# Layer 0 of a hybrid decoder: the second query chunk multiplied between the logits of two heads, and the output weights of the recurrent half split behind the heads' exponentials

## The chip, the cores and the metric

The kernel runs on one core of a Trainium2 chip. Its time is the device time of one execution in microseconds, the median of three runs. The core has TensorE (matrix products, into PSUM banks of 128x512 fp32), VectorE, ScalarE and GpSimd (elementwise work) and SyncE, which issues the DMAs. Each engine works through its own queue in order and waits at semaphores for the others.

## What is computed

A two-layer trunk over 512 positions of width 1024, in fp32. The change touches layer 0 alone:

```python
proj = x @ w_in          # 512 + 512 + 512 + 64 + 64 + 256 + 64 + 4 columns
xr, yr, q, k, v, iq, ik, iw = jnp.split(proj, split_points, axis=-1)
xr = causal_depthwise_conv(xr, conv_w, conv_b)
rec = rg_lru(xr, ...) * jax.nn.gelu(yr)          # recurrent half, 512 wide
att = dsa_attention(q, k, v, iq, ik, iw)         # 8 heads of 64; 128 best keys of each query
return jnp.concatenate([rec, att], axis=-1) @ w_out
```

`dsa_attention` scores all keys with the indexer (`iq`, `ik`, `iw`), keeps 128 of them for each query, and takes a causal softmax with a position bias over these. `rg_lru` is a gated linear recurrence over time. Then come a layer norm, a squared-ReLU MLP with a gated input embedding, and a second layer norm; layer 1 has latent attention in place of the hybrid mixer.

## The kernel before

Activations stand transposed, features on partitions and 512 positions along the free axis. A product that must be nearly fp32 is made of three matmuls in a faster fp32 format: weights and activations are split into a high and a low part (`split`, L88: ScalarE rounds to the high part, VectorE or GpSimd subtracts for the low part), and `mm3` adds high x high, high x low and low x high. `wload` (L92) loads a 1 MB chunk of weights into one of two `wraw` buffers and splits it into one of two `whi`/`wlo` pairs; `ahead` moves the split forward in the planner's priorities.

`mixer0` is layer 0's mixer. The input projection runs in chunks of 256 columns. Chunks 4 to 7 go through `gemm_full` (L591), which multiplies the raw fp32 weights by the raw `y` without any split, 16 matmuls for a chunk (the trace shows each as two records). Chunks 4 and 5 are the gelu branch; chunk 6 holds the queries of heads 0 to 3, chunk 7 those of heads 4 to 7. `ev3` (L670) evacuates a PSUM tile of two heads: for each head a ScalarE copy (L469), a VectorE difference (L470) and a second ScalarE copy (L673). `topk` (L542) runs on VectorE beside the chunks and gives the masks `mb`. `recurrence` (L638) and `recurrence_end` (L647) finish the recurrent half; the latter takes four blocks of 128 channels, two by two: (0, 1) before the attention, (2, 3) within it. A block of it is six VectorE instructions and a scan, one ScalarE scaling (L653), a cast to `mixed` (L89) and a subtraction on GpSimd (L90).

`attention` (L422) is a pipeline over the heads. In step i it traces the logits of head i, the transposes of head i - 2, the output of head i - 3, and then calls `after(i)`. `Head.logits` (L367) goes over four query blocks, 3 down to 0: two matmuls for each (L704, L705), then on VectorE one instruction that scales, masks and finds the extremum (L380). Blocks 1 and 0 share a PSUM bank, so the matmuls of block 0 wait until block 1 is masked. Then ScalarE takes four exponentials with their sums (L384), VectorE the reciprocals (L386), and GpSimd multiplies (the normalisation, L388, four instructions). The tiles of the sums have two buffers, so head i + 2's exponentials wait for head i's normalisation. `transposes` (L391) turns the probabilities by TensorE and splits them; `output` (L406) multiplies by the values.

`after(1)` traces `recurrence_end((2, 3))`, with its VectorE instructions queued behind head 1's last mask (`tc.issue_after`). `after(4)` and `after(6)` trace `gemm_t` of output-weight chunks 0 and 1, the recurrent half's: each loads and splits its chunk (on GpSimd for the low part) and makes 48 matmuls into the spare pair of PSUM banks (`ps_g`), which `ev_rec` adds to `y`. Chunks 2 and 3 follow after the attention.

A planner orders each engine's queue when the program is built: it runs through an estimate of time, and whenever an engine is free it issues the instruction of the highest priority that is ready. Priority is the order of tracing, moved by `ahead`. On the chip the queues then keep that order, whatever the real durations are.

Of the kernel before, what the change touches and what calls it, by code (L numbers as in the profile page):

```python
# [11 lines left out]
AF = mybir.ActivationFunctionType  # L12
OP = mybir.AluOpType

P = 128
# [38 lines left out]
def hybrid_kernel(ctx: ExitStack, tc: tile.TileContext, a: dict, out: bass.AP):  # L54
    nc = tc.nc
    uid = [0]

    def nm(s):
        uid[0] += 1
        return f"{s}_{uid[0]}"  # L60
# [18 lines left out]
    def ps_tile(tag=None):  # L79
        if tag is None:  # L80
            tag = TURN[turn[0] % 6]
            turn[0] += 1
        return psum.tile([P, S], F32, tag=tag, bufs=BANKS[tag], name=nm("ps"))

    def ps_g():
        return ps_tile("g")

    def split(hi, lo, src, act=None, sub=None):  # L88
        (act or nc.scalar.copy)(hi, src)  # L89
        (sub or nc.vector.tensor_sub)(lo, src, f(hi))  # L90

    def wload(dram, idx, n=2048, pieces=2, sub=None, raw=None, ahead=30):  # L92

        hi = wp.tile([P, 2048], F32R, tag="whi", name=nm("whi"))
        lo = wp.tile([P, 2048], F32R, tag="wlo", name=nm("wlo"))
        if raw is None:
            raw = wp.tile([P, 2048], F32, tag="wraw", name=nm("wraw"))
            nc.sync.dma_start(raw[:, :n], dram[idx, :, :n])
        m = n // pieces
        with tc.high_priority(ahead):  # L100
            for i in range(pieces):
                c = slice(i * m, (i + 1) * m)
                split(hi[:, c], lo[:, c], raw[:, c], sub=sub)
        return hi, lo

    def mm3(ps, whi, wlo, xhi, xlo, start, stop):
        nc.tensor.matmul(ps, whi, xhi, start=start, stop=False)  # L107
        nc.tensor.matmul(ps, whi, xlo, start=False, stop=False)  # L108
        nc.tensor.matmul(ps, wlo, xhi, start=False, stop=stop)  # L109

    ALL, HALVES = slice(0, S), (slice(0, H), slice(H, S))

    def gemm_t(dram, idxs, xs, evac, kk=8, nt=2, lead=0, ps=ps_tile, sub=None, loaded=None,
               halves=(), tail=0, ahead=30):

        tiles = {}  # L120

        def part(g, c, w, kn, cs=ALL):
            ktot = kk * len(idxs[g])
            for k, n in kn:
                key = g, n, cs.start
                if key not in tiles:
                    tiles[key] = ps()
                kx = c * kk + k
                hi, lo = xs[kx]
                o = slice((k * nt + n) * P, (k * nt + n + 1) * P)  # L130
                mm3(tiles[key][:, cs], w[0][:, o], w[1][:, o], hi[:, cs], lo[:, cs],
                    kx == 0, kx == ktot - 1)
                if kx == ktot - 1:
                    evac(g * nt + n, tiles[key], cs)

        first, last = 0, len(idxs) - tail
        byn = [(k, n) for n in range(nt) for k in range(kk)]
        byk = [(k, n) for k in range(kk) for n in range(nt)]
        if lead:
            w = loaded or [wload(dram, idxs[g][0], sub=sub, ahead=ahead) for g in range(2)]  # L140
            first = 2
            for cs in HALVES if "lead" in halves else (ALL,):
                for k in range(lead):
                    for g in range(2):
                        part(g, 0, w[g], [(k, n) for n in range(nt)], cs)
                for g in range(2):
                    kn = (byk, byn)[g]
                    part(g, 0, w[g], [t for t in kn if t[0] >= lead], cs)
        for g in range(first, last):
            for c, idx in enumerate(idxs[g]):  # L150
                part(g, c, wload(dram, idx, sub=sub, ahead=ahead), byn)
        if tail:
            w = {(g, c): wload(dram, idx, sub=sub, ahead=ahead) for g in range(last, len(idxs)) for c, idx in enumerate(idxs[g])}
            for cs in HALVES:
                for g in range(last, len(idxs)):
                    cn = [(c, n) for n in range(nt) for c in range(len(idxs[g]))]
                    for c, n in cn if cs.start == 0 else sorted(cn):
                        part(g, c, w[g, c], [(k, n) for k in range(kk)], cs)
# [201 lines left out]
    class Head:  # L360
# [6 lines left out]
        def logits(self):  # L367
            p = self.pool
            ps = {t: ps_tile("s") for t in "ABC"}
            sb = {t: p.tile([P, WIDTH[t]], F32, tag="l" + t, bufs=3 - (t in self.few), name=nm("l")) for t in "ABC"}  # L370
            mn = p.tile([P, NB], F32, tag="mn", name=nm("mn"))
            sums = p.tile([P, NB], F32, tag="sums", name=nm("sums"))
            L = {}
            for blk in (3, 2, 1, 0):
                t, c0 = S_AT[blk]
                n = (blk + 1) * P
                m = max(n, 2 * P)
                self.s_mm(ps[t][:, c0:c0 + m], blk, m)
                L[blk] = sb[t][:, c0:c0 + n]
                self.masked = nc.vector.tensor_tensor_reduce(  # L380
                    out=L[blk], in0=ps[t][:, c0:c0 + n], in1=self.mask(blk, n), scale=-self.scale,
                    scalar=-LOWEST, op0=OP.add, op1=OP.min, accum_out=mn[:, blk:blk + 1])
            for blk in (3, 2, 1, 0):
                nc.scalar.activation(L[blk], L[blk], AF.Exp, bias=mn[:, blk:blk + 1],  # L384
                                     scale=-1.0, accum_out=sums[:, blk:blk + 1])
            nc.vector.reciprocal(sums, sums)  # L386
            for blk in (3, 2, 1, 0):
                nc.gpsimd.tensor_scalar(L[blk], L[blk], sums[:, blk:blk + 1], 1.0, op0=OP.mult, op1=OP.mult)  # L388
            self.L = L
# [66 lines left out]
    def mixer0(mixed):  # L456
        with pool("m0", 1) as m0, pool("m0s") as sc:
# [4 lines left out]
            def scr():  # L462
                return sc.tile([P, S], F32, tag="s", bufs=1, name=nm("s"))
# [58 lines left out]
            for blk in (3, 2, 1):  # L522
                n = (blk + 1) * P
                isc[blk] = xp.tile([P, n], F32, tag=f"isc{blk}", bufs=1, name=f"isc{blk}")
                for h in range(4):
                    ps = ps_tile()
# [61 lines left out]
            gl = rp.tile([P, D], F32R, tag="gl", bufs=1, name="gl")  # L588
            split(gh, gl, gr[:, :D], sub=nc.gpsimd.tensor_sub)

            def gemm_full(idxs, evac):  # L591

                for g, idx in enumerate(idxs):
                    raw = wp.tile([P, 2048], F32, tag="wraw", name=nm("wraw"))
                    nc.sync.dma_start(raw, a["w_in"][idx])
                    for n in range(2):
                        ps = ps_tile()
                        for k in range(KT):
                            o = (k * 2 + n) * P
                            nc.tensor.matmul(ps, raw[:, o:o + P], y[k], start=k == 0, stop=k == KT - 1)  # L600
                        evac(2 * g + n, ps, ALL)
# [45 lines left out]
            def recurrence_end(ns):  # L647
                for n in ns:
                    T, rc, st, nt = rg[n], rcs[n], gy[n], scr()
                    nc.vector.scalar_tensor_tensor(nt, T, 1.0, rc, op0=OP.add, op1=OP.mult)  # L650
                    nc.vector.scalar_tensor_tensor(rc, nt, 2.0, rc, op0=OP.subtract, op1=OP.mult)
                    nc.vector.tensor_mul(T, T, rc)
                    nc.scalar.activation(T, T, AF.Copy, scale=2.0, bias=1.0)  # L653
                    nc.vector.tensor_mul(st, st, rc)
                    nc.vector.scalar_tensor_tensor(st, st, -1.0, ix[n], op0=OP.mult, op1=OP.mult)
                    nc.vector.tensor_tensor_scan(ix[n], T, st, 0.0, op0=OP.mult, op1=OP.add)
                    nc.vector.tensor_mul(gy[n], ix[n], gelu[n])
                    mixed[n] = new_h(n)
                    split(mixed[n][0], mixed[n][1], gy[n], sub=nc.gpsimd.tensor_sub)
# [12 lines left out]
                    head_halves(q1[:, 2 * n + j], ps, j)  # L672
                    nc.scalar.copy(q2[0:64, 2 * n + j], ps[64 * j:64 * j + 64])  # L673

            gemm_full([6, 7], ev3)
            recurrence()
            recurrence_end((0, 1))

# [4 lines left out]
            def ev_rec(n, ps, cs):  # L683
                nc.vector.scalar_tensor_tensor(y[n], y[n], ALPHA, ps, op0=OP.mult, op1=OP.add)

            def after(i):
                if i == 1:
                    with tc.issue_after(heads[1].masked.ins):
                        recurrence_end((2, 3))
                if i in (4, 6):  # L690
                    g = (i - 4) // 2
                    gemm_t(a["w_out0"], [[g]], mixed, lambda n, ps, cs: ev_rec(n + 4 * g, ps, cs), kk=4, nt=4,
                           ps=ps_g, sub=nc.gpsimd.tensor_sub)

            def mask(blk, n):
                return tri[:, 3 * P:] if blk == 0 else mb[blk]
# [1 line left out]
            heads = []  # L698
# [401 lines left out]
    for layer in range(2):  # L1100
        mixed = [None] * KT
# [111 lines left out]
```

## Time and profile before

| | us |
|---|---|
| time before, median of 3 runs | 1281.77 |
| lowest and highest of them | 1279.61, 1283.0 |
| the profiled execution's own time | 1281.88 |
| span of its trace | 1279.7 |
| TensorE busy | 1233.8 (96%) |
| VectorE busy | 936.5 (73%) |
| ScalarE busy | 685.3 (54%) |
| GpSimd busy | 161.7 (13%) |

The span runs from the first to the last instruction; 2.2 us lie around it. Busy times are of one profiled execution. Matmuls overlap one another in the records (a 128x512 matmul is shown as 0.39 us and the next starts 0.23 us later), so busy TensorE is not TensorE at its peak, and the spacing of starts is what a matmul costs. The granted clock is a share of 2.4 GHz; 0.50 is 1.2 GHz. Layer 0's mixer takes the first 210 us or so; the attention runs from about 122 to 205.

### The profile page before, as it was taken

How to read it: one execution, taken by the hardware profiler on the slowest of the kernel's cores; microseconds unless marked ns; L12 is line 12 of the kernel's file. 1: busy time of each engine (PE TensorE's matmuls, PEld its weight loads, DVE VectorE, ACT ScalarE, POOL GpSimd, SP SyncE). 2: the span in 40 equal slices, each digit the busy share in tenths (PEclk: the TensorE clock that was granted, in tenths of full speed). 3: DMA queues.
4: the chain of work that ended last, by engine and by line, in shares of the span. 5: the costliest groups of instructions: out<-in, count | busy, mean ns of one | idle time of the engine just before them, and what ended most of it. 6: DMA issues, size and time to landing. Idle time of an engine off the chain costs nothing.

```text
span 1279.7 us, 18724 instructions
## 1 busy us (share of the span) xinstructions
PE 1233.8 (96%) x7240; PEld 1066.5 (83%) x7240; DVE 936.5 (73%) x1833; ACT 685.3 (54%) x1260; POOL 161.7 (13%) x186
## 2 busy tenths in 40 slices
PE   7999699999999999999899999999999999999998
PEld 6744488989899899898787878899898998988987
DVE  5997677899667575585848888769985574855857
ACT  5593564756426245263366989636563262452633
POOL 0502651000000000000544443200000000000000
PEclk9999699999999999999998999999999999999999
DMA  6202112113223323233122110213232231332301
GB/s 215 100 34 95 69 34 83 67 66 132 100 99 103 119 75 123 72 103 131 35 71 99 34 34 1 83 66 100 99 100 99 99 132 66 100 130 68 132 33 67
DMA packets 20921, 110.96 MB, mean 87 GB/s; under 512 B 2464, under 2 KB 6560, under 8 KB 8640
## 3 DMA queue, kind: packets, MB, share of 16 engines
q1 hardware_dynamic: 20736, 109.18, 24.9%
q8 instruction: 56, 0.92, 0.3%
q0 software_dynamic: 96, 0.59, 0.2%
q14 instruction: 33, 0.27, 0.1%
HBM read 107.66 MB, written 2.10 MB: 86 GB/s over the span
## 4 chain that ended last, share of the span: by engine, by line
PE 76%; DVE 13%; ACT 6%; POOL 2%; issue 1%; DMA 1%; ACTq 0%; SPq 0%; POOLq 0%; DVEq 0%
PE ps L783 24%; PE ps L107 14%; PE ps L108 14%; PE ps L109 14%; DVE mb L551 2%; DVE m L550 2%; ACT whi L89 1%; PE ps L397 1%; ACT l L384 1%; POOL l L388 1%; PE ps L417 1%; PE ps L907 1%; PE ps L908 1%; PE ps L906 1%; POOL wlo L90 1%
## 5 line engine op out<-in xcount | busy, mean ns | idle before, releaser
L89 ACT CAST whi<-wraw 128x1024 fp32r<-128x1024 f32 (+3 forms) x154 | 129.9, 882 | 148.9 <-PE ps L108 113.9
L108 PE MATMUL ps<-al,whi 128*128 128x512 f32 (+1 forms) x544 | 206.4, 379 | 0.0
L107 PE MATMUL ps<-ah,whi 128*128 128x512 f32 (+1 forms) x544 | 206.4, 379 | 0.0
L109 PE MATMUL ps<-ah,wlo 128*128 128x512 f32 (+1 forms) x544 | 205.3, 377 | 0.0
L107 PE MATMUL ps<-hh,whi 128*128 128x256 f32 (+1 forms) x432 | 147.3, 344 | 8.2 <-ACT hh L89 6.6
L109 PE MATMUL ps<-hh,wlo 128*128 128x256 f32 (+1 forms) x432 | 145.5, 341 | 1.4 <-DVE wlo L90 0.8
L108 PE MATMUL ps<-hl,whi 128*128 128x256 f32 (+1 forms) x432 | 146.7, 341 | 0.1
L90 POOL TENSOR_TENSOR wlo<-wraw,whi 128x512 fp32r<-128x512 f32 (+2 forms) x46 | 73.3, 1614 | 484.4 <-ACT whi L89 452.6
L90 DVE TENSOR_TENSOR wlo<-wraw,whi 128x1024 fp32r<-128x1024 f32 (+1 forms) x108 | 116.1, 1107 | 16.5 <-ACT whi L89 16.3
L783 PE MATMUL ps<-xt,whi 128*128 128x256 f32 x680 | 124.6, 284 | 0.6 <-DVE u L802 0.6
L108 PEld LDWEIGHTS ps<-al,whi 128*128 128x128 f32 x544 | 102.8, 189 | 20.1 <-DVE al L90 1.2
L107 PEld LDWEIGHTS ps<-ah,whi 128*128 128x128 f32 x544 | 102.8, 189 | 19.6 <-ACT ah L89 1.1
L109 PEld LDWEIGHTS ps<-ah,wlo 128*128 128x128 f32 x544 | 102.7, 189 | 18.6 <-issue 0.5
L783 PEld LDWEIGHTS ps<-xt,whi 128*128 128x128 f32 x680 | 106.0, 192 | 1.0 <-DVE u L802 0.8
L748 ACT CAST whi<-wraw 128x1024 fp32r<-128x1024 f32 (+1 forms) x43 | 36.0, 836 | 130.1 <-PE ps L108 97.1
L874 DVE TENSOR_TENSOR y<-y,ps 128x512 f32<-128x512 f32 (+1 forms) x52 | 33.3, 644 | 94.2 <-PE ps L109 94.1
L107 PEld LDWEIGHTS ps<-hh,whi 128*128 128x128 f32 x432 | 82.5, 192 | 18.0 <-ACT hh L89 7.9
L783 PE MATMUL ps<-xt,wlo 128*128 128x256 f32 x340 | 96.2, 283 | 0.0
L109 PEld LDWEIGHTS ps<-hh,wlo 128*128 128x128 f32 x432 | 82.5, 192 | 10.9 <-DVE wlo L90 2.0
L108 PEld LDWEIGHTS ps<-hl,whi 128*128 128x128 f32 x432 | 83.0, 192 | 9.8 <-DVE hl L90 0.9
L783 PE MATMUL ps<-hh,wlo 128*128 128x256 f32 x260 | 73.5, 283 | 0.0
L783 PE MATMUL ps<-hl,whi 128*128 128x256 f32 x260 | 73.5, 283 | 0.0
(338 smaller groups left out, 2983.5 us busy)
## 6 DMA issues: line engine op xcount, KB each, us to landing
wraw<-in_mlp_w SPq DMA_DIRECT2D x64, 1024.0 KB, 4.8
wraw<-in_w_out SPq DMA_DIRECT2D x8, 1024.0 KB, 4.7
wraw<-in_w_gate SPq DMA_DIRECT2D x8, 1024.0 KB, 4.8
wraw<-in_w_in SPq DMA_DIRECT2D x6, 1024.0 KB, 4.8
wraw<-in_w_ukv SPq DMA_DIRECT2D x4, 1024.0 KB, 4.8
wraw<-in_w_in SPq DMA_DIRECT2D x16, 128.0 KB, 4.0
y<-in_xT SPq DMA_DIRECT2D x8, 256.0 KB, 3.8
wraw<-in_w_proj SPq DMA_DIRECT2D x2, 1024.0 KB, 4.8
```

The source lines that it names most:

```text
L89: (act or nc.scalar.copy)(hi, src)
L90: (sub or nc.vector.tensor_sub)(lo, src, f(hi))
L107: nc.tensor.matmul(ps, whi, xhi, start=start, stop=False)
L108: nc.tensor.matmul(ps, whi, xlo, start=False, stop=False)
L109: nc.tensor.matmul(ps, wlo, xhi, start=False, stop=stop)
L384: nc.scalar.activation(L[blk], L[blk], AF.Exp, bias=mn[:, blk:blk + 1], scale=-1.0, accum_out=sums[:, blk:blk + 1])
L388: nc.gpsimd.tensor_scalar(L[blk], L[blk], sums[:, blk:blk + 1], 1.0, op0=OP.mult, op1=OP.mult)
L550: nc.vector.max(out=m8, in_=src)
L551: nc.vector.match_replace(out=w, in_to_replace=m8, in_values=src, imm_value=LOWEST)
L748: nc.scalar.copy(hi, src)
L783: nc.tensor.matmul(o, u[:, c], v, start=start and k == n == 0, stop=k == 3 and n == 2, skip_group_check=True)
L874: nc.vector.tensor_add(yn, yn, ps[:, cs])
```

## The change

Chunk 7 is taken out of the call in front of `recurrence()`. It is multiplied in `after(1)` instead, traced behind the logits of head 1 and ahead of `recurrence_end((2, 3))`, and into the spare pair of PSUM banks. `gemm_full` gets the number of its first chunk and the banks as parameters for that. The output-weight chunks 0 and 1 are loaded and split in `after(1)` and `after(3)`; their ScalarE casts are queued behind the last exponential of head 1 and of head 3 (the instruction kept in `self.exp`), with `ahead=0`. `after(4)` and `after(6)` keep the same 48 matmuls each, in the same order.

```diff
-                nc.scalar.activation(L[blk], L[blk], AF.Exp, bias=mn[:, blk:blk + 1],
+                self.exp = nc.scalar.activation(L[blk], L[blk], AF.Exp, bias=mn[:, blk:blk + 1],
                                      scale=-1.0, accum_out=sums[:, blk:blk + 1])
...
-            def gemm_full(idxs, evac):
-
-                for g, idx in enumerate(idxs):
+            def gemm_full(idxs, evac, first=0, bank=ps_tile):
+
+                for g, idx in enumerate(idxs, first):
...
-                        ps = ps_tile()
+                        ps = bank()
...
-            gemm_full([6, 7], ev3)
+            gemm_full([6], ev3)
             recurrence()
             recurrence_end((0, 1))
...
             def after(i):
                 if i == 1:
+                    gemm_full([7], ev3, 1, ps_g)
                     with tc.issue_after(heads[1].masked.ins):
                         recurrence_end((2, 3))
+                if i in (1, 3):
+                    with tc.issue_after(heads[i].exp.ins):
+                        wo.append(wload(a["w_out0"], len(wo), sub=nc.gpsimd.tensor_sub, ahead=0))
                 if i in (4, 6):
                     g = (i - 4) // 2
-                    gemm_t(a["w_out0"], [[g]], mixed, lambda n, ps, cs: ev_rec(n + 4 * g, ps, cs), kk=4, nt=4,
-                           ps=ps_g, sub=nc.gpsimd.tensor_sub)
+                    for n in range(4):
+                        ps = ps_g()
+                        for k in range(4):
+                            o = slice((k * 4 + n) * P, (k * 4 + n + 1) * P)
+                            mm3(ps, wo[g][0][:, o], wo[g][1][:, o], *mixed[k], k == 0, k == 3)
+                        ev_rec(n + 4 * g, ps, ALL)
+
+            wo = []
```

## Rows read from the trace of the kernel before

**Rows 1.** The page's head: span, and each engine's busy time, share and instructions.
```profile
span 1279.7 us, 18724 instructions
PE 1233.8 (96%) x7240; PEld 1066.5 (83%) x7240; DVE 936.5 (73%) x1833; ACT 685.3 (54%) x1260; POOL 161.7 (13%) x186
```

**Rows 2.** Stretches 120 to 160 us: length, busy us by engine, clock, DMA.
```profile
120.00:125.00 5.00, 4.56 (x17) 2.72 (x16) 2.56 (x6) 2.68 (x5) 4.20 (x2) 1.00 0.00 0
125.00:130.00 5.00, 1.19 (x7) 0.67 (x5) 0.00 (x0) 1.13 (x2) 0.00 (x0) 1.00 0.98 369
130.00:135.00 5.00, 2.30 (x6) 1.92 (x7) 3.16 (x12) 4.93 (x8) 4.68 (x2) 0.63 0.13 52
135.00:140.00 5.00, 3.78 (x13) 3.00 (x11) 3.19 (x9) 3.81 (x15) 0.93 (x2) 0.69 0.64 210
140.00:145.00 5.00, 0.51 (x3) 0.51 (x4) 5.00 (x9) 1.16 (x2) 5.00 (x4) 0.65 0.00 0
145.00:150.00 5.00, 3.82 (x14) 2.97 (x12) 4.19 (x8) 3.97 (x11) 5.00 (x5) 0.50 0.00 0
150.00:155.00 5.00, 4.66 (x12) 2.74 (x11) 2.22 (x7) 1.11 (x3) 1.69 (x3) 0.50 0.00 0
155.00:160.00 5.00, 5.00 (x26) 4.50 (x24) 2.71 (x11) 2.70 (x8) 2.23 (x4) 0.64 0.00 0
```

**Rows 3.** Chain of waits that ended last, 119 to 149 us: start, us, what.
```profile
119.48 4.72 POOL wlo L90 x2
124.23 4.62 DMA wraw<-in_w_out
128.87 1.99 ACT whi L89 x2
...
139.07 10.30 POOL l L388 x8
```

**Rows 4.** TensorE's timeline: start, us, line, out<-in, count [idle before <- released by].
```profile
99.52 22.91 PE L600 MATMUL ps<-y,wraw 128*128 128x512 f32 x53
...
132.70 0.58 PE L704 MATMUL ps<-kx,q 128*128 128x256 f32 x1 [6.51 <-DVE mn L380]
...
144.49 2.40 PE L397 MATMUL ps<-cst,l 128*128 128x128 f32 x10 [5.71 <-POOL l L388]
...
148.49 1.22 PE L107 MATMUL ps<-hh,whi 128*128 128x512 f32 x2 [1.18 <-ACT hh L89]
```

**Rows 5.** VectorE's timeline, 104 to 138 us.
```profile
104.25 0.68 DVE L650 SCALAR_TENSOR_TENSOR s<-rg,rc 128x512 f32<-128x512 f32 x1
...
117.15 0.69 DVE L470 TENSOR_TENSOR q<-ps,q 64x512 fp32r<-64x512 f32 x1
...
123.64 0.69 DVE L380 CUSTOM_DVE_ANT_0 l<-ps,mb 128x512 f32<-128x512 f32 x1
...
137.38 0.69 DVE L650 SCALAR_TENSOR_TENSOR s<-rg,rc 128x512 f32<-128x512 f32 x1
```

**Rows 6.** ScalarE's timeline, 118 to 145 us.
```profile
118.36 1.99 ACT L89 CAST whi<-wraw 128x1024 fp32r<-128x1024 f32 x2
...
132.78 0.72 ACT L384 ACTIVATE l<-l,mn 128x512 f32<-128x512 f32 x1
...
144.47 0.72 ACT L384 ACTIVATE l<-l,mn 128x512 f32<-128x512 f32 x1 [3.51 <-POOL l L388]
```

**Rows 7.** GpSimd's timeline, 119 to 175 us.
```profile
119.48 4.71 POOL L90 TENSOR_TENSOR wlo<-wraw,whi 128x1024 fp32r<-128x1024 f32 x2 [0.37 <-ACT whi L89]
...
130.05 4.68 POOL L90 TENSOR_TENSOR wlo<-wraw,whi 128x1024 fp32r<-128x1024 f32 x2 [5.85 <-ACT whi L89]
...
161.37 2.07 POOL L388 TENSOR_SCALAR l<-l,sums 128x512 f32<-128x512 f32 x4 [4.14 <-PE ps L397]
...
172.72 2.41 POOL L90 TENSOR_TENSOR wlo<-wraw,whi 128x1024 fp32r<-128x1024 f32 x1 [5.10 <-ACT whi L89]
```

**Rows 8.** The page's DMA issues: KB each, us from issue to landing.
```profile
wraw<-in_w_out SPq DMA_DIRECT2D x8, 1024.0 KB, 4.7
```

## The prediction

> **What bounds the kernel now.** The page first: TensorE is busy for 96% of the span [rows 1], so in nearly all of the kernel only less TensorE work would help, and the change takes none away. What is left is the 4% in which TensorE idles, and the stretches in which it runs at the lower clock. The table by stretches shows where the change can reach: between 120 and 160 us, the first 40 us of layer 0's attention, TensorE is busy for only 25.8 of 40 us [rows 2]. The idle rest, stretch by stretch, is 0.44 + 3.81 + 2.70 + 1.22 + 4.49 + 1.18 + 0.34 + 0 = **14.2 us**. The granted clock falls to 0.63 and 0.50 of full speed there; busy time times the missing share (2.30 x 0.37 + 3.78 x 0.31 + 0.51 x 0.35 + 3.82 x 0.50 + 4.66 x 0.50 + 5.00 x 0.36) is **8.2 us** lost to 1.2 instead of 2.4 GHz (the clock of a row is a mean over its five us, so this is good to a us or two). Together 22.4 us: the ceiling of what this change can win, since before and behind that stretch TensorE is full.
>
> Why it idles is told by the chain of waits, read downwards. ScalarE casts the first output weights at 118.4 [rows 6]; GpSimd subtracts for 4.7 us [rows 3]; only then does the chain reach the DMA of the second output weights, 4.6 us in which ScalarE stands at the head of its in-order queue with a cast whose data have not come; that cast takes 2.0 us; and the exponentials of head 0, whose first masked logits were on VectorE at 123.64 [rows 5], start at 132.78 [rows 6]. TensorE meanwhile stands 6.51 us at the fourth logits block of head 0, which waits for VectorE's mask of the third block (they share a bank) [rows 4]. Next on the chain is GpSimd's normalisation of heads 0 and 1, eight instructions in 10.3 us [rows 3], for which TensorE's first transposes wait 5.71 us [rows 4].
>
> **The change, part by part.**
>
> *Query chunk 7 behind the logits of head 1.* Its 16 fp32 matmuls are 32 records; 53 of them take 22.91 us [rows 4], so 0.43 us each and 13.8 us for the chunk. None is removed. The chunk leaves the place at 108.5 to 122.4, where TensorE was full, and heads 0 and 1, whose queries come from chunk 6, follow chunk 6 directly. It becomes cover for the softmax of head 0. The eight copies and four differences that evacuate it move along, at the same cost. Its DMA keeps its place in SyncE's queue, ahead of the output weights. Its two PSUM tiles come from the spare pair of banks: costed at nothing, because the output matmuls that use this pair are now later than the chunk; if that cover were gone, they would wait for one evacuation, about 1.3 us.
>
> *Output weights behind the exponentials.* The same four casts and four subtractions, some 4 us of ScalarE [rows 3, 6] and 9.4 us of GpSimd [rows 7], but the casts of the first now queue behind head 1's exponentials and those of the second behind head 3's. So the 4.6 us DMA wait leaves the path: by head 3 the second weights, 4.7 us from issue to landing [rows 8], have long come. Behind the casts stand head 2's exponentials, and these wait 3.51 us for GpSimd's normalisation of head 0 already [rows 6], so 2 us of casts hide there; without that cover they cost 2 us. On GpSimd the subtractions now come between the normalisations of successive heads.
>
> *The schedule that results.* I go by engine order. (a) Chunk 6 ends at 108.5; TensorE issues three logits blocks of head 0, one or two of head 1, and a little of chunk 7. The fourth block of head 0 still waits for VectorE. VectorE is in the first half of the recurrence until 117.85, with the differences of heads 2 and 3 in it: eighteen rows from 104.25 to 117.15, none with idle time before it [rows 5]; three masks are 1.6 us more. If the masks stand behind all that, TensorE can go on at 119.5, having stopped at 112 or 113. **A stall of 6 us remains** (0, if the masks get in between, to 8). I take 6: the row of the same wait in the kernel before says 6.51. (b) After that wait TensorE ran at the lower clock for some 5 us [rows 2]: **2.5 us** lost again (0 to 4). (c) Then chunk 7 runs on, with the remaining logits of heads 0 to 2, about 14 us in all: TensorE is covered to 136. Head 0's exponentials run from about 119, not 132.78; with head 1's normalisation they bring GpSimd's eight instructions to 123 to 133.7, if they are as slow as before. So both sets of transposes are ready when TensorE comes to them, and the 5.71 us wait and the 1.18 us behind it are gone. (d) TensorE has the two sets of transposes, then needs output matmuls: the first output weights are whole on GpSimd at 133.7 + 4.8 = 138.5, TensorE is there at about 138.5 too, and waits for masks of head 2 behind the second half of the recurrence. **A gap of 2 us** (0 to 5), nearest to the 1.18 us row [rows 4], with **1.4 us** of lower clock behind it (0 to 5, the worst being half of the ten us at 0.50 [rows 2]). From there 48 output matmuls are ready as filling.
>
> What is left of the 22.4 us is 6 + 2.5 + 2 + 1.4 = 11.9, so the gain is 10.5 us. The profiled execution took 1281.88 us, 0.1 from the median of the runs and 2.2 more than its span [rows 1]: 1281.9 - 10.5 = **1271.4 us**. With the ends of each term 0 to 22 us are left; ends of all terms together are unlikely, and 5 to 17 is the forecast's own range, 1265 to 1277.
>
> *A rule against it.* The eight normalisations that took 10.3 us [rows 3] ran while VectorE was in the second half of the recurrence, from 137.38 on [rows 5]; later, without it, four took 2.07 [rows 7], so eight would take 4.1. The Trainium skill (SBUF — State Buffer, section Who interferes with whom) says that a VectorE instruction with two SBUF inputs contends with a GpSimd instruction that reads SBUF, and that whichever comes second is blocked until the other is done. By it the subtractions of the first output weights, which had VectorE nearly to themselves at 119.5 to 124.2 and 130.0 to 134.7, would be drawn out like the normalisations; by their own rows they stay at 2.35 us apiece [rows 7].
>
> **The rivals.**
>
> *Slower: the split stands in the softmax.* The subtractions of the first output weights are drawn out beside the recurrence by the ratio of the normalisations, 10.3 / 4.1 = 2.5: 11.9 instead of 4.8 us, 7.1 more, all of it ahead of head 2's normalisation and of the output matmuls. If the second's 4.8 us also hold up head 4's normalisation with TensorE idle, and the lower clock lasts another ten us (5 us), then 11.9 + 7.1 + 4.8 + 5 = 28.8 us are lost where 22.4 are lost now: 1288 us. It decides once those waits exceed 10.5 us together. For it: GpSimd is busy 5.0 of 5 us at 140 to 150 [rows 2]. Against: the same kind of split at 160 to 186 stood between normalisations at 2.41 us apiece [rows 7], and TensorE, with output matmuls to fill, stayed full.
>
> *The bubble only moves.* The first stall is 8 us with 4 of low clock, and the gap of (d) 5 with 4: 21 of the 22.4 us. 1280.5 us, no change that can be measured.
>
> *The masks get in between.* VectorE has the masks of head 0 between the differences of heads 2 and 3: no first stall and no lower clock, 8.5 us more, of which 1 to 2 us go to waiting for GpSimd: 1264 us. For it: a chain on one engine has latencies to fill. Against: the eighteen rows without a gap [rows 5].
>
> *The move does not happen.* Nothing holds chunk 7 back: its operands are there by 100 us, and it may be issued ahead of the logits, which wait for ScalarE and VectorE. Then only the weights' part counts: the exponentials start where the masks allow, 123.64 plus about a us instead of 132.78, some 8 us, of which the first output matmuls, which now come later, give back 2: 1275.5 us.
>
> **How the numbers follow.** Forecast 0.55, masks in between 0.15, no move 0.09, bubble moves 0.12, slower 0.09. About 0.3%, 3.8 us, is what a measurement of this kernel can tell from no change. Below 1278: nearly all of the forecast, the second and most of the third, 0.78; within: the moved bubble and edges, 0.13; slower 0.09. The range takes the forecast's own with the case of 1264 below and most of the moved bubble above: 1263 to 1280; outside are the slower case and small tails, under 2 in 10.
>
> **What would show it.** Right: the fp32 matmuls of chunk 7 standing between the logits of heads 1 and 2; the first exponential at 117 to 121; no DMA in ScalarE's waits; TensorE's wait for the normalisations gone; one wait of some 6 us for VectorE's mask. Wrong: chunk 7 directly behind chunk 6; transposes waiting for GpSimd behind a subtraction; or a TensorE that is not full from 140 to 180, which would mean that the latency of the softmax bounds the stage and the cover won at its start is paid at its end.

## The result, and the profile after

The changed kernel takes **1274.46 us** (median of 7 runs, 1272.04 to 1278.69) against 1281.77 us for the kernel before (7 runs, 1279.61 to 1284.62): 7.3 us less, a ratio of 0.9946, with 0.9932 to 0.996 as its 95% interval. The prediction was 1271.4, within 1263 to 1280. The direction and most of the mechanism hold; the gain is 7.3 us where 10.5 were forecast.

The profiled execution is the slowest of the seven (1278.69 us). The page's head, which answers to [rows 1]:

```profile
span 1276.7 us, 18725 instructions
PE 1233.9 (97%) x7240; PEld 1068.4 (84%) x7240; DVE 941.2 (74%) x1833; ACT 684.7 (54%) x1260; POOL 157.7 (12%) x186
```

This span is a poor measure of the change: it holds some 4 us lost far behind it, in layer 1. The table by stretches shows that (us; then busy us of TensorE, its weight load, VectorE, ScalarE, GpSimd, each with its instructions; granted clock; DMA share; GB/s). First before, then after:

```profile
600.00:620.00 20.00, 19.02 (x108) 16.09 (x106) 19.52 (x25) 9.74 (x15) 6.41 (x4) 1.00 0.16 53
620.00:640.00 20.00, 15.97 (x89) 14.31 (x89) 16.15 (x39) 7.48 (x17) 10.51 (x12) 0.91 0.17 57
640.00:660.00 20.00, 19.90 (x107) 17.25 (x108) 11.14 (x33) 11.96 (x34) 10.48 (x16) 1.00 0.15 55
```

```profile
600.00:620.00 20.00, 17.04 (x104) 16.05 (x103) 16.33 (x28) 6.56 (x13) 6.39 (x4) 0.85 0.12 43
620.00:640.00 20.00, 17.88 (x89) 15.63 (x88) 14.76 (x35) 6.66 (x16) 10.50 (x12) 0.84 0.09 31
640.00:660.00 20.00, 20.00 (x108) 17.57 (x107) 8.79 (x25) 12.94 (x35) 10.74 (x16) 0.97 0.25 77
```

TensorE is busy for 54.9 us of these 60 in both (the same work lies some 7 us earlier after the change), but at a clock of 0.85 and 0.84 instead of 1.00 and 0.91. So I compare the stage by two marks of its own: from the first fp32 matmul of `gemm_full` (L600: at 64.53 us before, 65.35 after) to the first matmul of the layer norm behind the attention (L261). That is TensorE's timeline of before, then of after (start, us, engine, line, tile, count):

```profile
221.16 0.63 PE L261 MATMUL ps<-n_s,cst 128*128 128x256 f32 x2
```

```profile
214.37 0.63 PE L261 MATMUL ps<-n_s,cst 128*128 128x256 f32 x2
```

The **stage** takes 221.16 - 64.53 = 156.6 us before and 149.0 after: 7.6 us less, close to the 7.3 of the medians. The stretches of after that answer to [rows 2]:

```profile
110.00:115.00 5.00, 3.01 (x10) 1.41 (x9) 4.93 (x8) 2.38 (x4) 0.60 (x1) 1.00 0.64 210
115.00:120.00 5.00, 2.15 (x4) 1.48 (x5) 4.85 (x9) 4.20 (x8) 1.12 (x1) 0.57 0.00 0
120.00:125.00 5.00, 5.00 (x14) 2.55 (x13) 2.21 (x12) 3.11 (x12) 2.36 (x3) 0.75 0.00 2
125.00:130.00 5.00, 5.00 (x13) 2.23 (x12) 4.87 (x10) 3.92 (x10) 4.28 (x6) 1.00 0.00 0
130.00:135.00 5.00, 5.00 (x21) 3.00 (x20) 4.94 (x5) 1.76 (x4) 5.00 (x4) 1.00 0.00 0
135.00:140.00 5.00, 0.27 (x3) 0.03 (x1) 4.93 (x4) 1.17 (x3) 3.64 (x2) 0.96 0.42 129
140.00:145.00 5.00, 3.70 (x11) 3.01 (x12) 4.88 (x9) 4.01 (x9) 0.00 (x0) 0.50 0.69 290
145.00:150.00 5.00, 5.00 (x28) 4.30 (x27) 3.79 (x16) 3.99 (x12) 2.48 (x3) 0.86 0.00 0
```

Read as before, TensorE's idle time is 1.99 + 2.85 + 4.73 + 1.30 = 10.9 us, and its busy time at the missing share of the clock (2.15 x 0.43 + 5.00 x 0.25 + 0.27 x 0.04 + 3.70 x 0.50 + 5.00 x 0.14) is 4.7 us: 15.6 us lost where 22.4 were. The loss has two holes, one at 113 to 118 and one at 135 to 141. TensorE's timeline names them (in brackets the idle time before, and what ended it):

```profile
111.27 1.88 PE L600 MATMUL ps<-y,wraw 128*128 128x512 f32 x4
117.84 0.69 PE L714 MATMUL ps<-kx,q 128*128 128x384 f32 x1 [4.70 <-DVE mn L380]
...
124.70 8.75 PE L600 MATMUL ps<-y,wraw 128*128 128x512 f32 x20
...
134.34 0.93 PE L397 MATMUL ps<-cst,l 128*128 128x128 f32 x7
141.30 0.90 PE L397 MATMUL ps<-cst,l 128*128 128x128 f32 x3 [6.03 <-DVE mn L380]
```

Chunk 7 stands between the logits, its bulk behind those of head 1. The row of 117.84 is head 1's second block, which needs the bank that head 0's first mask frees. The wait for the normalisations of [rows 4] (5.71 us) is gone: seven transposes of head 0 run at 134.34 with no wait at all. But the last three need a PSUM bank that head 2's first mask frees, and that mask comes late, though head 2's first logits ran at 132.88: late queries are not the cause. ScalarE, which answers to [rows 6], and GpSimd, to [rows 3, 7]:

```profile
118.24 0.72 ACT L384 ACTIVATE l<-l,mn 128x512 f32<-128x512 f32 x1
```

```profile
123.92 2.99 POOL L388 TENSOR_SCALAR l<-l,sums 128x512 f32<-128x512 f32 x4 [2.51 <-DVE sums L386]
127.62 4.25 POOL L388 TENSOR_SCALAR l<-l,sums 128x512 f32<-128x512 f32 x4 [0.72 <-DVE sums L386]
131.85 5.12 POOL L90 TENSOR_TENSOR wlo<-wraw,whi 128x1024 fp32r<-128x1024 f32 x2
136.93 1.71 POOL L90 TENSOR_TENSOR hl<-gy,hh 128x512 fp32r<-128x512 f32 x1
```

The first exponential starts at 118.24, 14.5 us earlier. Head 0 and 1 are normalised in 7.2 us, not 10.3. Then come the subtractions of the first output weights, 131.85 to 136.97. VectorE, first at the mask that ends the first hole, then beside these subtractions:

```profile
117.12 0.66 DVE L380 CUSTOM_DVE_ANT_0 l<-ps,mb 128x512 f32<-128x512 f32 x1
...
132.46 2.30 DVE L657 TENSOR_TENSOR gy<-ix,gelu 128x512 f32<-128x512 f32 x1
134.69 2.83 DVE L651 SCALAR_TENSOR_TENSOR rc<-s,rc 128x512 f32<-128x512 f32 x1
137.55 1.64 DVE L652 TENSOR_TENSOR rg<-rg,rc 128x512 f32<-128x512 f32 x1
...
140.54 0.69 DVE L380 CUSTOM_DVE_ANT_0 l<-ps,mb 128x512 f32<-128x512 f32 x1
```

Three instructions of the recurrence's second half, 0.69 us each elsewhere [rows 5], take 2.30, 2.83 and 1.64 us. Behind them and two more of the recurrence stands the mask (140.54) for which TensorE waits.

### The profile page after: what moved, and what is told of

The parts are those of the page before. It is cut to its first block, busy times and chain, and to the rows that moved or that the text cites. A ratio compares the mean times of both kernels' runs of the same rounds, so it can differ in the third digit from the quotient of the medians.

```text
span 1276.7 us, 18725 instructions
## 1 busy us (share of the span) xinstructions
PE 1233.9 (97%) x7240; PEld 1068.4 (84%) x7240; DVE 941.2 (74%) x1833; ACT 684.7 (54%) x1260; POOL 157.7 (12%) x186
## 4 chain that ended last, share of the span: by engine, by line
PE 80%; DVE 12%; ACT 6%; issue 1%; POOL 1%; DMA 0%; ACTq 0%; SPq 0%; DVEq 0%
PE ps L793 25%; PE ps L107 15%; PE ps L108 15%; PE ps L109 15%; DVE mb L551 2%; DVE m L550 2%; PE ps L397 1%; ACT l L384 1%; ACT whi L89 1%; PE ps L417 1%; PE ps L917 1%; PE ps L918 1%; PE ps L916 1%; DVE xc L611 1%; DVE isc L536 1%
```

## The experiments

The theory after this reading: both parts of the change do one thing, which is to start head 0's exponentials earlier; the second hole is VectorE's queue, in which the recurrence stands ahead of head 2's masks and is drawn out beside GpSimd's subtractions. Rivals: it is the chunk's place that brings the gain; the second hole is late queries; or GpSimd's order is what bounds. "Layer norm at" is its first matmul in the profiled execution, of which the expectations speak; "stage" is the time between the two marks, which takes out that the first mark itself lies at 64.5 to 66.3 us; the rest of the kernel scatters by some 4 us (median less stage is 1125 to 1129 us in all of these). Each ratio is to runs of the kernel before taken beside it (their medians are 1281.77 to 1282.48 us).

The stage is read from a single execution of each kernel, and one thing in it varies by itself. Near the end of the attention every one of these kernels has one more wait of TensorE for a normalisation, 1.82 to 1.86 us (at 189.31 in the change). In the five us behind it the granted clock is 0.66 in six traces (before, the change, the chunk alone, the second weights alone, the low part on VectorE, both masks early with the low part on VectorE) and 1.00 in the other eight; that is 1.7 us of busy TensorE. I therefore read no difference of the stage below 2 us as an effect by itself.

| kernel | median, us | ratio to before | layer norm at | stage, us | against before |
|---|---|---|---|---|---|
| before | 1281.77 | | 221.16 | 156.6 | |
| the change | 1274.46 | 0.9946 [0.9932, 0.996] | 214.37 | 149.0 | -7.6 |
| chunk alone | 1277.41 | 0.9955 [0.9939, 0.997] | 215.63 | 149.3 | -7.3 |
| weights alone | 1275.41 | 0.9949 [0.9933, 0.9964] | 212.91 | 147.1 | -9.5 |
| second weights alone | 1273.64 | 0.9947 [0.9932, 0.9962] | 214.21 | 148.1 | -8.5 |
| low part on VectorE | 1273.24 | 0.9926 [0.9909, 0.9942] | 210.39 | 145.1 | -11.5 |
| mask before last block | 1271.67 | 0.9914 [0.9897, 0.993] | 208.43 | 143.6 | -13.0 |
| first mask early | 1272.28 | 0.9918 [0.9903, 0.9933] | 210.61 | 144.6 | -12.0 |
| both masks early | 1273.49 | 0.9932 [0.9917, 0.9948] | 211.45 | 146.7 | -10.0 |
| both, low part on VectorE | 1278.12 | 0.9963 [0.9949, 0.9977] | 216.11 | 150.2 | -6.5 |
| both, chunk back in front | 1288.35 | 1.0043 [1.0029, 1.0057] | 225.63 | 159.4 | +2.8 |
| last block and low part | 1273.41 | 0.9932 [0.9906, 0.9959] | 209.90 | 144.3 | -12.4 |
| chunk and last block | 1274.47 | 0.9948 [0.9928, 0.9968] | 211.25 | 145.1 | -11.5 |
| chunk in two halves | 1279.94 | 0.9973 [0.996, 0.9987] | 218.45 | 152.5 | -4.1 |

**The two parts, each alone.** The kernel before with chunk 7 moved:

```diff
-            gemm_full([6, 7], ev3)
+            gemm_full([6], ev3)
...
                 if i == 1:
+                    gemm_full([7], ev3, 1, ps_g)
```

> Chunk 7 moved, output weights loaded and split as in the kernel before. Theory: the gain is the cover that the chunk gives the softmax of heads 0 and 1. Once the chunk is moved, ScalarE and GpSimd are busy with these heads when the first output weights could be split, so the casts queue behind head 1's exponentials without being told to: 1274.5, within 2 us of the full change, the first exponential near 118 and no wait of ScalarE for a DMA in the attention. Rival (the DMA wait was the loss, and only the weights' part removes it): the wait of 4 to 5 us on ScalarE is back and the time is 1278 to 1280.

The same two holes (4.70 and 6.04 us) and the same stage within 0.3 us: with the chunk moved, the planner puts the first weights' cast behind head 1's exponentials anyway. The theory's mechanism came (first exponential at 119.21 us, no wait of ScalarE for a DMA). Its time did not: 1277.41 is almost 3 us above the full change, where within 2 was forecast, though the intervals of the two ratios overlap.

The kernel before with the splits moved (the 48 matmuls of a chunk written out as in the change) and the chunk in front:

```diff
+                if i in (1, 3):
+                    with tc.issue_after(heads[i].exp.ins):
+                        wo.append(wload(a["w_out0"], len(wo), sub=nc.gpsimd.tensor_sub, ahead=0))
```

> Output weights split behind the exponentials of heads 1 and 3, chunk 7 left in front of the attention. Theory: exponentials of head 0 start near 125.5 in place of 132.8, but TensorE has neither chunk 7 nor early output matmuls to cover the softmax: its idle time in the first 40 us of the attention stays above 10 us, and the time is 1276 to 1280. Rival (the weights' part carries the gain): 1274.5 or below.

1275.41 us lies between the two forecasts. The stage gains 9.5 us, 1.9 more than with both parts; 1.7 of that is the clock behind the late wait, and by the ratios the chunk alone, the weights alone and both can't be told apart. TensorE's idle time stays above 10 us, as forecast; its waits are those of before with the exponentials earlier, at 125.60 (TensorE, then GpSimd):

```profile
136.31 2.40 PE L397 MATMUL ps<-cst,l 128*128 128x128 f32 x10 [7.52 <-POOL l L388]
...
143.51 0.50 PE L109 MATMUL ps<-hh,wlo 128*128 128x512 f32 x1 [3.09 <-POOL wlo L90]
```

```profile
130.89 10.26 POOL L388 TENSOR_SCALAR l<-l,sums 128x512 f32<-128x512 f32 x8 [10.53 <-DVE sums L386]
```

The two parts are substitutes. Each takes the waiting cast from ahead of the exponentials; the second to be added brings nothing that these runs can tell from noise, because the hole that it would close opens elsewhere.

**Which cast.** The split of the second output weights alone moved behind head 3's exponentials, the first left where it was:

```diff
+                if i == 1:
+                    wo.append(wload(a["w_out0"], 0, sub=nc.gpsimd.tensor_sub, ahead=30))
+                if i == 3:
+                    with tc.issue_after(heads[3].exp.ins):
+                        wo.append(wload(a["w_out0"], 1, sub=nc.gpsimd.tensor_sub, ahead=0))
```

> The kernel before with one thing changed: the split of the second output weights is queued behind head 3's exponentials. Chunk 7 stays in front and the first output weights keep their early split. First theory (what the weights' part removes is the ScalarE cast that stands waiting for its DMA ahead of the exponentials, and nothing else): the whole gain of the weights' part is here, first exponential at about 124 to 126 instead of 132.8, layer norm's first matmul behind the attention at 212 to 214, 1275 to 1277 us. Rival (the first output weights' cast and subtractions ahead of the softmax cost as well, so that half of the gain needs both splits moved): layer norm at 216 to 218, 1278 to 1280 us.

8.5 of the 9.5 us are here, and by the ratios (0.9947 and 0.9949) all of it (1273.64 us, a little under the forecast; the layer norm at 214.21, a little above). The first exponential, on ScalarE's timeline, comes 5.1 us earlier than in [rows 6], later than forecast because evacuations of chunk 7 and the first weights' casts (2 us) still stand ahead of it:

```profile
127.70 0.72 ACT L384 ACTIVATE l<-l,mn 128x512 f32<-128x512 f32 x1
```

So the loss that the weights' part removes is the second split, and in it the cast that stood 4.6 us waiting for its DMA. The split's subtractions were not in the way: in the kernel before they ended at 134.73 [rows 7], and GpSimd's normalisation waited until 139.07 for VectorE. The same cast was also behind TensorE's 6.51 us of [rows 4]. Ahead of the mask that TensorE waited for, VectorE stood for a ScalarE copy (at 130.88) that is queued behind the cast (VectorE, before):

```profile
131.50 0.68 DVE L470 TENSOR_TENSOR q<-ps,q 64x512 fp32r<-64x512 f32 x1 [6.68 <-ACT q L469]
```

Whether the first weights' early split cost anything by itself these runs don't show; the difference is one microsecond of the stage.

**The second hole.** The changed kernel with the first output weights' low part subtracted on VectorE:

```diff
-    wo.append(wload(a["w_out0"], len(wo), sub=nc.gpsimd.tensor_sub, ahead=0))
+    wo.append(wload(a["w_out0"], len(wo), sub=None if i == 1 else nc.gpsimd.tensor_sub, ahead=0))
```

> The full change, with the two subtractions of the first output weights on VectorE instead of GpSimd. Theory: the second wait of TensorE (6.0 us, a bank that head 2's first mask must free) is made by three VectorE instructions of the recurrence that took 6.8 us beside these subtractions where 2.0 are usual. Without them on GpSimd the three take 0.7 us each, the wait shrinks by 3 to 5 us (VectorE has 2.2 us of subtractions more, some of it ahead of the mask), time 1269 to 1272. Rival (order alone: the mask stands behind the recurrence, and what it is beside does not matter): the wait stays at 5 to 6 us, 1274 to 1276.

VectorE's timeline, then TensorE's waits:

```profile
131.84 0.69 DVE L657 TENSOR_TENSOR gy<-ix,gelu 128x512 f32<-128x512 f32 x1
132.45 0.69 DVE L651 SCALAR_TENSOR_TENSOR rc<-s,rc 128x512 f32<-128x512 f32 x1
...
134.18 1.77 DVE L652 TENSOR_TENSOR rg<-rg,rc 128x512 f32<-128x512 f32 x1
```

```profile
137.14 0.50 PE L417 MATMUL ps<-p,v 128*128 128x512 f32 x1 [2.05 <-ACT p L89]
138.66 0.91 PE L397 MATMUL ps<-cst,l 128*128 128x128 f32 x3 [0.56 <-DVE mn L380]
```

With GpSimd's subtractions gone from beside them the same instructions are back at 0.69, and the wait of 6.03 us is down to 2.61 in two pieces. The one that still overlaps a GpSimd subtraction (`hl`) takes 1.77, and the piece of 2.05 goes back to it: the ScalarE cast that TensorE waits for stands behind a scaling that waits for this instruction. Only 0.56 is the mask's. The drawing out is shown. The time, 1273.24, is 1.2 us above the forecast.

The changed kernel with the recurrence's last block behind head 2's masks:

```diff
-                        recurrence_end((2, 3))
+                        recurrence_end((2,))
+                if i == 2:
+                    with tc.issue_after(heads[2].masked.ins):
+                        recurrence_end((3,))
```

> The full change, with the last block of the recurrence traced behind head 2's masks and queued behind them on VectorE; the subtractions stay on GpSimd. Theory: head 2's first mask no longer waits for the last block, so it comes when its logits are there (134) and not at 140.5; the wait of 6.0 us falls below 1.5 us, and the lower clock behind it goes: 1267 to 1271. Rival (the drawing-out moves with the work and holds up something else, the last part of the recurrence, which the output matmuls need): TensorE stops for 4 to 6 us before those matmuls instead, 1273 to 1276.

```profile
136.27 0.73 PE L717 MATMUL ps<-kx,q 128*128 128x512 f32 x2 [0.81 <-DVE mn L380]
```

TensorE's timeline has the second hole at 0.81 us and the first as it was (4.69); 1271.67 us is 0.7 above the theory's range. All ten transposes of head 0 now run without a wait. So the hole needed both, the order and the drawing out, and goes with either. By its median this is the fastest kernel of the study, and it is faster than the changed one, since the intervals of the two ratios don't overlap. Both edits on one kernel:

> The changed kernel with the recurrence's last block behind head 2's masks and the first output weights' low part subtracted on VectorE. First theory (both edits take away the same second wait, of TensorE for a mask of head 2, so they do not add up): 1270 to 1273 us, the layer norm's first matmul at 207 to 210, as with the block's place alone (1271.7, 208.4). Rival (the small waits left there, 0.59, 0.70 and 1.40 us, are drawn out subtractions too and go as well): 1268.5 to 1270 us, layer norm at 205.5 to 207. Second rival (with GpSimd free earlier, the second output weights' subtractions get ahead of the last block's on GpSimd, and the output matmuls wait for it): 1274 to 1278 us, with a TensorE wait of over 1.5 us for the low part of the recurrence's last block.

They do not add up: waits of 0.82, 0.59, 0.69 and 1.39 us, as with the block's place alone (0.81, 0.59, 0.70, 1.40). The time, 1273.41, is 0.4 us above the first theory's range, the layer norm within it. And the block's place with the weights split as in the kernel before:

> The kernel before with chunk 7 behind the logits of head 1 and the recurrence's last block behind head 2's masks; the output weights are split as in the kernel before. First theory (with the chunk in its new place the weights' part is worth a us or so, as 215.6 against 214.4 said): layer norm's first matmul at 208.5 to 210.5, 1272 to 1274.5 us. Rival (the later split of the weights is what lets the edit pay, since it keeps GpSimd free for the normalisations): layer norm at 212 or later, 1275.5 to 1278 us.

1274.47 us is at the upper edge of the first theory; the layer norm at 211.25 lies between the two theories. The medians are 2.8 us apart, the stages 1.5, and the intervals of the ratios overlap a little: the weights' part is probably worth one to three microseconds once the chunk stands behind head 1 and the mask ahead of the last block.

**The first hole.** The changed kernel with the recurrence's second block behind head 0's masks:

```diff
-            recurrence_end((0, 1))
+            recurrence_end((0,))
...
+                if i == 0:
+                    with tc.issue_after(heads[0].masked.ins):
+                        recurrence_end((1,))
```

> The full change, with the second block of the recurrence traced behind head 0's masks and queued behind them on VectorE. Theory: the masks of head 0 come 3 to 4 us earlier and TensorE's first wait of 4.7 us falls below 1 us. But VectorE is busy 4.9 of 5 us from 100 to 120 and from 125 to 145, and the masks of head 2 stay behind all four blocks: TensorE only comes sooner to its second wait, which grows by what the first loses, but for the 2.8 us that VectorE idled between 120 and 125: 1271 to 1274. Rival (the two waits are separate losses): the second stays at 6 us and the time falls by 4.7 us and the 2 us of lower clock behind it: 1267 to 1269.

```profile
113.59 0.56 PE L717 MATMUL ps<-kx,q 128*128 128x384 f32 x1 [1.37 <-DVE mn L380]
...
141.18 0.90 PE L397 MATMUL ps<-cst,l 128*128 128x128 f32 x3 [4.92 <-DVE mn L380]
```

The first wait falls to 1.37 us: VectorE's order was its cause. The time is the theory's, 1272.28; its mechanism came in part. TensorE now stops twice before the last transposes, 2.73 us for the recurrence's low part on GpSimd and 4.92 for the mask, 7.65 where 6.03 were. So 1.6 of the 3.3 us won come back at the second hole, and the rest is kept. Then both order edits:

> The masks of head 0 ahead of the second block and those of head 2 ahead of the fourth block of the recurrence. Theory (VectorE is what bounds this stretch once TensorE has cover): the work in front of head 2's masks is the same as with these masks alone mended, so only VectorE's idle 2.8 us at 120 to 125 are to be had: 1268 to 1271, 1 to 3 us below that kernel. Rival (separate losses): 6 to 7 us below it, 1265.

Missed. It is worse than the last block's place alone. The second hole is back, on TensorE's timeline, and VectorE's shows why:

```profile
135.53 0.90 PE L397 MATMUL ps<-cst,l 128*128 128x128 f32 x3 [5.50 <-DVE mn L380]
```

```profile
127.12 2.74 DVE L655 SCALAR_TENSOR_TENSOR gy<-gy,ix 128x512 f32<-128x512 f32 x1
129.96 3.18 DVE L656 TENSOR_TENSOR_SCAN ix<-rg,gy 128x512 f32<-128x512 f32 x1
133.17 1.57 DVE L657 TENSOR_TENSOR gy<-ix,gelu 128x512 f32<-128x512 f32 x1
```

Behind the second block, which was pushed back, the third one now lies beside the subtractions of the output weights (126.95 to 132.06), and still ahead of head 2's mask. Taking these subtractions off GpSimd as well:

> As with both masks early, and the subtractions of the first output weights on VectorE. Theory: VectorE, the bound, has 2.2 us more work and is relieved of the blocking by GpSimd, which costs it 3 to 5 us where the recurrence is beside the subtractions: 0 to 3 us faster than without, 1266 to 1270. Rival (GpSimd's subtractions no longer touch the path once the masks come early): the 2.2 us are added, 1270 to 1273.

Missed by more than the rival allowed. The waits for masks shrink (3.31 instead of 5.50 us), but the planner now puts the second weights' subtractions on GpSimd ahead of the last block's low part, which the output matmuls need (GpSimd):

```profile
152.07 4.71 POOL L90 TENSOR_TENSOR wlo<-wraw,whi 128x1024 fp32r<-128x1024 f32 x2
156.74 1.26 POOL L90 TENSOR_TENSOR hl<-gy,hh 128x512 fp32r<-128x512 f32 x1
```

TensorE is busy for 7.1 of the ten us from 150 to 160, where it had 8.6 without this edit. Over the whole stage it idles as long as without it (11.7 us against 12.1), but in more pieces. By five-us stretches from the first mark, 7.6 us are lost to the lower clock where 3.4 were: 1.7 behind the late wait, the rest behind these pieces.

**Is the chunk's place needed at all?** Both order edits and the new splits, with chunk 7 back in front:

> As with both masks early, but chunk 7 back in front of the attention; the output weights stay behind the exponentials. Theory: without the chunk as cover TensorE waits again for the first softmax, 7 to 8 us for GpSimd's normalisation, as with the weights alone: 1274 to 1276. Rival (the order of the masks carries the gain, not the place of the chunk): within 2 us of the kernel with both masks early.

Missed, and the only kernel slower than before. Head 0's logits now come 13.7 us later (counted from the first mark), and the recurrence's blocks are bound to stay behind the masks of these logits, so VectorE stands empty (third busy figure: 1.38 and 1.10 of 5 us; with the weights alone, where only the chunk stands in front, 3.95 and 2.18):

```profile
115.00:120.00 5.00, 5.00 (x13) 2.20 (x12) 1.38 (x2) 3.43 (x6) 0.00 (x0) 1.00 0.00 0
120.00:125.00 5.00, 5.00 (x17) 2.69 (x16) 1.10 (x2) 1.48 (x4) 0.00 (x0) 1.00 0.00 0
```

So with both order edits it is the early logits, which the chunk's place allows, that make them pay. The last block's place alone, with the chunk in front, was not tried.

**Work in the first hole.** The last block's place, and chunk 7 in two halves, one ahead of head 1's logits:

```diff
+                if i == 0:
+                    gemm_full([7], ev3, 1, ps_g, tiles=(0,))
                 if i == 1:
-                    gemm_full([7], ev3, 1, ps_g)
+                    gemm_full([7], ev3, 1, ps_g, raw=last[-1], tiles=(1,))
```

> The changed kernel with the recurrence's last block behind head 2's masks, as in an earlier run (layer norm's first matmul at 208.4, 1271.7 us), and chunk 7 cut in two: its first eight matmuls stand ahead of head 1's logits, the second eight behind them, so that TensorE has 6.9 us of work where it stood 4.69 us for VectorE's masks. First theory (that stall is lost time and any work at its place wins it, with the lower clock behind it): the wait of 4.69 is under 1.5 us, layer norm at 202.5 to 206, 1266 to 1269 us. Rival (VectorE's queue sets the pace there, so that TensorE, earlier by 4 us, waits as much longer for head 2's masks or for the normalisation): a new wait of over 2 us between 125 and 140 us, layer norm at 206.5 to 210, 1270 to 1273 us.

Both theories missed (TensorE, then VectorE):

```profile
120.82 0.58 PE L724 MATMUL ps<-kx,q 128*128 128x256 f32 x1 [5.38 <-DVE mn L380]
121.41 5.32 PE L603 MATMUL ps<-y,wraw 128*128 128x512 f32 x6
```

```profile
127.25 0.69 DVE L380 CUSTOM_DVE_ANT_0 l<-ps,mb 128x512 f32<-128x512 f32 x1 [4.56 <-PE ps L725]
```

Only ten of the half's sixteen records get ahead; then TensorE waits 5.38 us for a mask as before, now with head 1's logits behind it and behind six more records at the lower clock (0.50). VectorE waits 4.56 us for these logits, and all that is queued behind their masks is later: the stage is 8.9 us longer than with the chunk whole. Filling TensorE by delaying logits costs more than the hole here.

## Why the prediction was right in direction and 3.1 us too low

- **The ceiling and its reading** held: 22.4 us lost before, 15.6 after. By the same sum the gain is 6.8 us; the two marks say 7.6, the medians 7.3. One part of it was wrong: TensorE is not full all the way behind 160 us. A wait for a normalisation stands at 196.13 before (1.86 us) and at 189.31 after (1.84 us), which the change does not touch.
- **The move** happened as predicted, and the case of no move did not come. What came lies between the forecast and the bubble that only moves, which had a second gap of 5 us. The no-move case, worked out at 1275.5 us, is in effect the kernel with the weights' part alone: 1275.41. That the two agree so well is partly luck, since its sum gave 6.4 us and the stage gained 9.5.
- **The first exponential** was put at about 119 and came at 118.24, with no DMA in ScalarE's waits and both normalisations ahead of their transposes: step (c) held, and the DMA wait left the path. The second weights moved alone show that this one wait is nearly all of the weights' part.
- **(a), (b), the first hole**: 6 us predicted, 4.70 measured; 2.5 us of lower clock predicted, 0.92 + 1.25 = 2.2 found. VectorE's order was the cause; the kernel with head 0's masks earlier shows it. The smaller size is a piece of the case of masks in between. Head 0's first mask (117.12) got ahead of the last difference and the last product of the recurrence's first half, 1.4 us of VectorE. The row of 6.51 that (a) leaned on had another cause, ScalarE's wait for the DMA, so its nearness to 6 was luck.
- **(d), the second hole, is the term that was mis-sized.** The waiter was named rightly, masks of head 2 behind the second half of the recurrence, but the gap was set at 2 us, by the nearest row of 1.18 [rows 4], with 1.4 us of lower clock. It took 6.03 us, above the 0 to 5 given, with 1.85 + 0.7 = 2.6 of lower clock: 5.2 us too little, of which (a) and (b) gave 1.6 back. That is nearly the whole miss of 3.7 us in the sum.
- **Where those us are.** By (d)'s own times the gap ran from 138.5 to 140.5; it ran from 135.27 to 141.30. At its start (d) let both sets of transposes go ahead of the wait. Only seven of the twenty could: three need the bank that head 2's first mask frees, and head 1's ten, traced behind the logits of head 3, run from 148.33. So what the first hole gave back was waited away at the second. At its end (d) never added up VectorE's queue, which decides when the mask comes.
- **VectorE's queue was longer by a price that stood in the prediction, on the wrong side.** I asked whether GpSimd's subtractions would be drawn out beside the recurrence; they were not by much, 2.56 us apiece instead of 2.35. It was VectorE that paid: 6.8 us for three instructions that take 2.1. The Trainium skill (SBUF — State Buffer, section Who interferes with whom) says that it depends on the order of issue which of the two blocks. These traces agree: the VectorE instruction that began at 132.46, 0.61 us into the first subtraction, took 2.30 us instead of 0.69. I had weighed only one of the two directions, and the price belonged in (d), since VectorE holds the masks.
- **The slower rival** did not come: the split stood in the softmax, but 48 output matmuls covered the rest, and TensorE is full from 145 to 185.

What stays open: why layer 1's start runs at a lower clock in some executions (0.85 and 0.84 against 1.00 and 0.91 at the same 54.9 us of work). Behind the second mark the trace of the kernel before is the shortest of all fourteen, 1058.5 us against 1059.4 to 1062.5, and there is one trace of each. So either that execution was a lucky one, or the changed kernels give back some of what they win; the stage can overstate a gain by as much as 4 us, and the ratios are the safer measure. The kernel with the chunk in two halves spreads from 1274.88 to 1283.0 us over 11 runs. No run was made for either.

## What to carry to other kernels

Look for a cast or copy that waits for a DMA at the head of an in-order queue in front of work that is ready; moving the split that holds it was worth 8.5 us of the stage here (a ratio of 0.9947), and two ways of taking the wait away did not add up. When a split or subtraction is moved on GpSimd, price it on VectorE too, and add up VectorE's queue to the mask or evacuation that TensorE waits for, also to the one that frees a PSUM bank. Work that covers a latency belongs behind the instructions that start that latency: ahead of them, as the chunk in two halves shows, it lengthens the chain by more than it fills.

## What the runs showed of the hardware that was not expected

VectorE instructions with two SBUF inputs, 0.69 us alone, took 1.57 to 2.85 us beside GpSimd subtractions of about 2.56 us each (2.85 with the first mask early), and a scan of 1.22 to 1.46 us took 3.18 with both masks early; GpSimd's own instructions grew by a tenth there (5.12 against 4.7 us for two). In the other pairing the cost fell on GpSimd: with the weights alone eight normalisations took 10.26 us beside the recurrence, where four without it take 2.07 [rows 7]. In the change, the row in which the wait of 4.70 us ends has a granted clock of 0.57 and the next 0.75; for the wait of 6.03 us they are 0.50 (1.2 GHz) and 0.86. TensorE was full ahead of both (100 to 110 and 125 to 135 us). Behind the wait of 1.8 us near the end of the attention the clock fell in six traces and not in eight.
